# A two-layer diffusion block on one core: GpSimd keeps only powers, first weight pieces used two at a time, head norms in two steps

## The chip, the core and the metric

The kernel runs on one core of a Trainium2 chip. The core has five engines that run side by side: TensorE (PE in the profile) multiplies matrices, VectorE (DVE) and GpSimd (POOL) do arithmetic on tiles, ScalarE (ACT) does functions and copies, and SyncE (SP) issues DMAs. Each engine works through its own queue in order; semaphores hold an instruction until its inputs are there and its output buffer is free. The metric is device time in microseconds of one execution of the whole kernel.

## The reference

A stream of 256 latent tokens (`lat`) and one of 256 context tokens (`cx`), both 1024 wide, pass through two layers. Each layer is an FFN, a mixer and another FFN, each on the RMS-normed and modulated stream, with a gated addition behind it:

```python
for layer in range(DEPTH):                       # DEPTH = 2
    lat = macaron(lat, g[0], mod_l, 0, *f0)      # h + 0.5*gate*swiglu(adaln_in(h))
    cx = macaron(cx, g[0], mod_c, 0, *f0)
    h_l, h_c = adaln_in(lat, g[1], mod_l, 1), adaln_in(cx, g[1], mod_c, 1)
    y_l, y_c = mixer_ab(...) if layer % 2 == 0 else mixer_c(...)
    lat = macaron(lat + mod_l[:, 5] * y_l, g[2], mod_l, 2, *f1)
    if need_ctx:
        cx = macaron(cx + mod_c[:, 5] * y_c, g[2], mod_c, 2, *f1)
return rmsnorm(lat, final_norm_w)
```

`mixer_ab` (layer 0) has four heads of differential attention with rotary positions, whose outputs are RMS-normed per head (`rmsnorm(o, subln_w) * (1 - lam_init)`), and beside it a Hyena branch: a short convolution of three taps, then two long convolutions by Fourier transform with gates. `mixer_c` (layer 1) has 16 heads of neighbourhood attention with a position bias `rpb` on the latent keys. The modulation `mod` is a product of `silu(c)` with a 1024 x 9216 matrix in each layer. All data is float32.

## The kernel before

Tokens lie along the free axis: `res[d]` holds 128 channels of 512 tokens, latent in columns 0 to 255 and context in 256 to 511. Every float32 product is made of three products of a reduced type: `split` (L149) rounds a tensor to `hi` on ACT and takes `lo = src - hi` on another engine, and `mm3` (L154) issues hi*hi, hi*lo and lo*hi. Weights come in as raw tiles by DMA (`wload`, L494, three buffers) and are split in pieces of 128 output columns by `whalf` (L487) into the pools `whi` and `wlo`, four buffers each.

What the program writes is put into an order on each engine by a planner that has its own estimate of each instruction's cost; source order counts as priority. So neighbours in the source can be found mixed on an engine.

- **FFN** (`ffn`, L526). Eleven blocks of 256 hidden columns. For block 0, `ffn_first` (L521) loads w1 and w3 and makes four pieces (w1 and w3 of columns 0 to 127, then of 128 to 255), and `products` (L512) goes over the eight channel blocks k, all four pieces at each k, first for the latent stream, then for the context stream. Where `ffn` calls `ffn_first` itself, `lo` of these pieces is computed on GpSimd (L580). The very first FFN gets its pieces made earlier, on VectorE (L1087). The other blocks go piece by piece (`up`), and `down` adds the second product to `res` (L510).
- **Between blocks.** `after` is called behind the last products of each stream: `Adaln.stream` (L467) makes the next `h` from `res`. `token_rs` (L431) squares `res[d]` on ACT, adds up on VectorE (L439), sums over channels with matmuls by `ones` (L443, L444) and takes the power -1/2 on GpSimd (L447); `token_rstd` spreads it with a matmul (L455). `h` has eight buffers in the H pool.
- **mixer_ab** (L678). Projections alternate with heads of attention. `emit_qk` (L700) applies the rotation: multiplication by cos on GpSimd (L710), by sin on VectorE. `norms` (L863) norms two heads: squares and their sums (L868, L870), the power on GpSimd (L874), matmuls that spread it (L879), the product and its split. It is called for heads 0 and 1 behind `project_v` and the tables, and for heads 2 and 3 behind the first `spectrum`. `conv2` (L843) leaves its result in `zb`, four tiles of the H pool, which the last `out_project` reads. The M pool (six buffers) holds `v`, the tokens `vy` of the long convolutions, and the second FFN weights.
- **mixer_c** (L926). `position` (L960) loads a head's bias by two DMAs and adds the mask on GpSimd (L967), in the pool T of ten buffers; `scores` adds it to the scores on VectorE (L986).

Of the kernel before, what the change touches and what calls it, by code (L numbers as in the profile page):

```python
# [10 lines left out]
F32 = mybir.dt.float32  # L11
# [7 lines left out]
P = 128  # L19
# [78 lines left out]
def tile_dit(ctx: ExitStack, tc: tile.TileContext, a: dict, out: bass.AP, dbg=None):  # L98
# [49 lines left out]

    def split(hi, lo, src, eng=V):  # L149

        S.activation(hi, src, AF.Copy)  # L151
        eng.tensor_tensor(lo, src, hi.bitcast(F32), op=ALU.subtract)  # L152

# [332 lines left out]

    def whalf(src, name, shape=(8, P), eng=V):  # L487

        hi = wp.tile([P, *shape], F32R, tag="whi", name=name + "h")
        lo = wp.tile([P, *shape], F32R, tag="wlo", name=name + "l")  # L490
        split(hi, lo, src, eng)
        return hi, lo
# [27 lines left out]

    def ffn_first(l, j, eng=V):  # L521

        r1, r3 = [wload(a[nm][l, j][:, :FB]) for nm in ("ffn_w1", "ffn_w3")]
        return [whalf(r[:, :, P * c : P * c + P], "w", eng=eng) for c in range(2) for r in (r1, r3)]

    def ffn(l, j, streams, ad, mods, after, ws=None):  # L526
# [52 lines left out]
        n = len(streams)  # L579
        ws = ws or ffn_first(l, j, nc.gpsimd)  # L580
        first = [PU() for _ in range(4)]
        for s in streams:
            products(first, ws, h, span([s]))
        for b in range(NFB):
# [93 lines left out]
    def mixer_ab(ad, mods, after):  # L678
# [21 lines left out]
        def emit_qk(o):  # L700
            def emit(i, ps):
                i += o
                scale = 0.125 if i < 4 else 1.0
                hi, lo = qk[i] = G(name="qk")
                u, sw = X("u"), X("sw")
                S.activation(u, ps[:, :LAT], AF.Copy, scale=scale)
                S.activation(hi[:, LAT:], ps[:, LAT:], AF.Copy, scale=scale)
                V.scalar_tensor_tensor(lo[:, LAT:], ps[:, LAT:], scale, hi[:, LAT:].bitcast(F32), op0=ALU.mult, op1=ALU.subtract)
                V.stream_shuffle(sw, u, list(range(16, 32)) + list(range(16)))
                nc.gpsimd.tensor_tensor(u, u, cosT, op=ALU.mult)  # L710
                V.tensor_tensor(sw, sw, sinT, op=ALU.mult)
                V.tensor_tensor(u, u, sw, op=ALU.add)
                split(hi[:, :LAT], lo[:, :LAT], u)
            return emit
# [128 lines left out]
        def conv2(s, pinv=PS):  # L843
# [3 lines left out]
            for ch in range(4):  # L847
# [9 lines left out]
                if s == 0:  # L857
                    zb.append(H(name="z"))
                split(zb[ch][0][:, sl], zb[ch][1][:, sl], x)
# [3 lines left out]
        def norms(hds):  # L863
# [9 lines left out]
            V.tensor_scalar(rs[:, :n], st[:, :n], 1.0 / P, EPS, op0=ALU.mult, op1=ALU.add)  # L873
            nc.gpsimd.tensor_tensor(rs[:, :n], rs[:, :n], nhalf[:, :n], op=ALU.pow)  # L874
            for i, hd in enumerate(hds):
                bc = PS()
# [5 lines left out]
                za.append(G(name="z"))  # L882
                split(*za[hd], x)

        project_first(win, (0, 512), h, (emit_qk(0), emit_qk(4)))
# [9 lines left out]
        load_tokens("hv", 1)  # L895
        project(win, 1792, 2, h, emit_hy(2), PD)
        project_v(win, 1280, h, emit_v(1), PD)
        tab = [wp.tile([P, 2, TOK], F32R, tag=("whi", "wlo", "wlo")[i], name="tab") for i in range(3)]
# [3 lines left out]
        for o in range(2):  # L902
            nc.sync.dma_start(tn[o][1:], TR[o][0][1:])
            nc.sync.dma_start(tn[o][0:1], TN[o])
        norms((0, 1))
        head(2)
        project(win, 2048, 2, h, emit_hy(4), PD)
        head(3)
        load_filters(0)
        project(win, 2304, 2, h, emit_hy(6), PD)  # L910
        spectrum(PU, "hv", 0, 0)
        norms((2, 3))
        conv1(0)
# [12 lines left out]
    def mixer_c(ad, mods, after):  # L926
# [33 lines left out]
        def position(hd):  # L960
# [3 lines left out]
            for r2 in range(2):  # L964
                src = bass.AP(tensor=rpb.tensor, offset=hd * 465 + (5 - r2) * 31 - 48, ap=[[1, 64], [31, 6], [1, 64]])
                nc.sync.dma_start(b3[64 * r2 : 64 * r2 + 64], src)
            nc.gpsimd.tensor_tensor(b3, b3, mask, op=ALU.add)  # L967
            return b
# [192 lines left out]
```

## Time and profile before

| | us |
|---|---|
| median of 3 runs (1901.84 to 1902.35) | 1902.21 |
| the profiled execution | 1902.08 |
| its span | 1900.3 |
| PE busy | 1850.6 (97%) |
| VectorE busy | 1257.0 (66%) |
| ScalarE busy | 738.0 (39%) |
| GpSimd busy | 73.6 (4%) |

The profile has a row for each group of instructions: line of the kernel, engine, operation, tile names (out<-in), shapes, count, then busy time and mean duration in ns, then the engine's idle time in front of the group and what ended it. Views of single instructions give start and duration in us. A window's row gives the length, the busy time of PE, its weight loads, VectorE, ScalarE and GpSimd with instruction counts, and then the clock granted to TensorE as a share of full speed. A matmul's end is modelled, and matmuls overlap, so spacing from start to start tells more than duration.

### The profile page before, as it was taken

How to read it: one execution, taken by the hardware profiler on the slowest of the kernel's cores; microseconds unless marked ns; L12 is line 12 of the kernel's file. 1: busy time of each engine (PE TensorE's matmuls, PEld its weight loads, DVE VectorE, ACT ScalarE, POOL GpSimd, SP SyncE). 2: the span in 40 equal slices, each digit the busy share in tenths (PEclk: the TensorE clock that was granted, in tenths of full speed). 3: DMA queues.
4: the chain of work that ended last, by engine and by line, in shares of the span. 5: the costliest groups of instructions: out<-in, count | busy, mean ns of one | idle time of the engine just before them, and what ended most of it. 6: DMA issues, size and time to landing. Idle time of an engine off the chain costs nothing.

```text
span 1900.3 us, 25792 instructions
## 1 busy us (share of the span) xinstructions
PE 1850.6 (97%) x10358; PEld 1566.0 (82%) x10358; DVE 1257.0 (66%) x1972; ACT 738.0 (39%) x1190; POOL 73.6 (4%) x63
## 2 busy tenths in 40 slices
PE   7999999999999998999999999999999999989998
PEld 3868788889878788888888897887888988889998
DVE  5557686776666795877767358655344866667665
ACT  4533233224555433432332234222322566654443
POOL 1000000000100002000000110000000100020000
PEclk9999999999999999999999999999999999989998
DMA  8675555351323332545554325443323233335551
GB/s 267 216 245 177 171 186 208 127 191 45 122 88 100 104 109 84 195 170 175 197 184 143 111 78 176 173 160 113 111 89 119 54 106 84 106 111 178 200 188 57
DMA packets 191009, 271.65 MB, mean 143 GB/s; under 512 B 19688, under 2 KB 139755, under 8 KB 190889
## 3 DMA queue, kind: packets, MB, share of 16 engines
q1 hardware_dynamic: 189324, 267.63, 42.7%
q10 hardware_dynamic: 1260, 2.14, 0.3%
q8 instruction: 81, 1.33, 0.3%
q14 instruction: 40, 0.32, 0.1%
q0 software_dynamic: 304, 0.24, 0.0%
HBM read 262.63 MB, written 7.34 MB: 142 GB/s over the span
## 4 chain that ended last, share of the span: by engine, by line
PE 67%; DVE 4%; ACT 2%; issue 1%; POOL 1%; DMA 0%; SPq 0%; DVEq 0%; ACTq 0%
PE pu L155 11%; PE pu L156 11%; PE pu L157 11%; PE pd L155 7%; PE pd L157 7%; PE pd L156 7%; PE ps L155 3%; PE ps L156 3%; PE ps L157 3%; PE pu L1012 1%; DVE wl L152 1%; PE ps L667 1%; DVE acc L439 1%; PE pu L982 1%; PE ps L293 1%
## 5 line engine op out<-in xcount | busy, mean ns | idle before, releaser
L157 PE MATMUL pu<-h,wl 128*128 128x512 f32 (+1 forms) x1600 | 545.6, 342 | 3.0 <-POOL wl L152 3.0
L155 PE MATMUL pu<-h,wh 128*128 128x512 f32 (+1 forms) x1600 | 545.0, 342 | 1.6 <-ACT h L483 1.5
L156 PE MATMUL pu<-h,wh 128*128 128x512 f32 (+1 forms) x1600 | 546.0, 342 | 0.1
L151 ACT ACTIVATE wh<-raw 128x1024 fp32r<-128x1024 f32 x228 | 240.3, 1058 | 558.6 <-PE pu L156 403.2
L152 DVE TENSOR_TENSOR wl<-raw,wh 128x1024 fp32r<-128x1024 f32 x216 | 263.7, 1225 | 203.8 <-ACT wh L151 177.6
L155 PEld LDWEIGHTS pu<-h,wh 128*128 128x128 f32 x1600 | 303.8, 191 | 44.1 <-issue 4.2
L157 PEld LDWEIGHTS pu<-h,wl 128*128 128x128 f32 x1600 | 304.7, 191 | 38.4 <-POOL wl L152 3.3
L156 PEld LDWEIGHTS pu<-h,wh 128*128 128x128 f32 x1600 | 304.9, 191 | 33.8 <-DVE h L484 0.5
L282 DVE SCALAR_TENSOR_TENSOR mv<-mw,sF,mv 128x1024 f32<-128x1024 f32 x210 | 258.5, 1279 | 20.5 <-DMA mw<-in_mod_w_dram 16.2
L151 ACT ACTIVATE w<-raw 128x1024 fp32r<-128x1024 f32 x88 | 91.5, 1057 | 164.2 <-PE ps L156 120.5
L510 DVE SCALAR_TENSOR_TENSOR res<-pd,gate,res 128x256 f32<-128x256 f32 x244 | 110.7, 479 | 40.5 <-PE pd L157 40.0
L547 DVE TENSOR_TENSOR sg<-sg,pu 128x512 f32<-128x512 f32 (+1 forms) x87 | 52.2, 603 | 127.4 <-PE pu L157 125.0
L152 DVE TENSOR_TENSOR w<-raw,w 128x1024 fp32r<-128x1024 f32 x88 | 107.0, 1221 | 42.0 <-ACT w L151 41.9
L155 PE MATMUL pd<-g,w 128*128 128x512 f32 (+1 forms) x376 | 133.6, 355 | 0.0
L157 PE MATMUL pd<-g,w 128*128 128x512 f32 (+1 forms) x376 | 132.6, 353 | 0.0
L156 PE MATMUL pd<-g,w 128*128 128x512 f32 (+1 forms) x376 | 132.6, 353 | 0.0
L155 PE MATMUL ps<-g,w 128*128 128x512 f32 (+1 forms) x320 | 116.3, 363 | 0.0
L157 PE MATMUL ps<-g,w 128*128 128x512 f32 (+1 forms) x320 | 116.1, 363 | 0.0
L156 PE MATMUL ps<-g,w 128*128 128x512 f32 (+1 forms) x320 | 116.1, 363 | 0.0
L155 PE MATMUL pd<-h,wh 128*128 128x512 f32 (+1 forms) x288 | 108.3, 376 | 1.9 <-ACT e L989 0.9
L157 PE MATMUL pd<-h,wl 128*128 128x512 f32 (+1 forms) x288 | 107.6, 374 | 1.7 <-DVE wl L152 1.7
L156 PE MATMUL pd<-h,wh 128*128 128x512 f32 (+1 forms) x288 | 106.9, 371 | 0.0
(256 smaller groups left out, 2726.0 us busy)
## 6 DMA issues: line engine op xcount, KB each, us to landing
raw<-in_ffn_w_dram SPq DMA_DIRECT2D x132, 1024.0 KB, 5.3
mw<-in_mod_w_dram SPq DMA_DIRECT2D x144, 512.0 KB, 6.0
raw<-in_ab_w_in_dram SPq DMA_DIRECT2D x12, 1024.0 KB, 6.9
raw<-in_na_w_in_dram SPq DMA_DIRECT2D x12, 1024.0 KB, 5.0
raw<-in_ab_w_out_dram SPq DMA_DIRECT2D x4, 1024.0 KB
raw<-in_na_w_out_dram SPq DMA_DIRECT2D x4, 1024.0 KB, 5.5
bias<-in_na_rpb_dram SPq DMA_DIRECT2D x32, 96.0 KB, 6.1
dftr<-const_dft_dram SPq DMA_DIRECT2D x5, 256.0 KB
```

What stands on the lines that cost most here:

```text
L151: S.activation(hi, src, AF.Copy)
L152: eng.tensor_tensor(lo, src, hi.bitcast(F32), op=ALU.subtract)
L155: nc.tensor.matmul(ps, wh, xh, start=start, stop=False)
L156: nc.tensor.matmul(ps, wh, xl, start=False, stop=False)
L157: nc.tensor.matmul(ps, wl, xh, start=False, stop=stop)
L282: V.scalar_tensor_tensor(acc, mw, c, acc, op0=ALU.mult, op1=ALU.add)
L293: nc.tensor.matmul(ps[32 * j : 32 * j + 32], row[:, 31 - b : 63 - b], mod_acc[l, i][j % 2][:, j // 2], start=b == 0, stop=b == len(batch) ...
L439: V.tensor_tensor(acc, acc, q, op=ALU.add)
L510: V.scalar_tensor_tensor(res[d][:, sl], ps[:, po], g[:, d, s : s + 1], res[d][:, sl], op0=ALU.mult, op1=ALU.add)
L547: V.tensor_tensor(sg[:, sl], sg[:, sl], p3[:, sl], op=ALU.mult)
L667: nc.tensor.transpose(at[kt // 2][:, o : o + P], e[:, P * kt : P * kt + P], ident)
L982: nc.tensor.matmul(pss[m], x[pr, qsl], y[pr], start=n == 0, stop=n == 2)
```

## The change

`split`, `whalf` and `ffn_first` lose their engine parameter, so `lo` of the four first pieces of three FFNs is computed on VectorE; the multiplication by cos and the addition of the mask move there too. GpSimd then computes only the powers (L447, L874). The first products of an FFN go through two pieces (columns 0 to 127 of w1 and w3) for all k, then through the other two. `zb` is taken from the M pool. `norms` becomes a generator with two steps: squares, sums and power; then, at its second call, the spreading, product and split. The first step is now called one projection (`project_v`, or `project` at 2304 with a `spectrum`) ahead of the second, which stays in place.

```diff
--- before.py
+++ after.py
@@ -146,10 +146,10 @@
     V = nc.vector
     S = nc.scalar
 
-    def split(hi, lo, src, eng=V):
+    def split(hi, lo, src):
 
         S.activation(hi, src, AF.Copy)
-        eng.tensor_tensor(lo, src, hi.bitcast(F32), op=ALU.subtract)
+        V.tensor_tensor(lo, src, hi.bitcast(F32), op=ALU.subtract)
 
     def mm3(ps, wh, wl, xh, xl, start, stop):
         nc.tensor.matmul(ps, wh, xh, start=start, stop=False)
@@ -484,11 +484,11 @@
                 V.scalar_tensor_tensor(lo[:, sl], x, B, hi[:, sl].bitcast(F32), op0=ALU.add, op1=ALU.subtract)
 
 
-    def whalf(src, name, shape=(8, P), eng=V):
+    def whalf(src, name, shape=(8, P)):
 
         hi = wp.tile([P, *shape], F32R, tag="whi", name=name + "h")
         lo = wp.tile([P, *shape], F32R, tag="wlo", name=name + "l")
-        split(hi, lo, src, eng)
+        split(hi, lo, src)
         return hi, lo
 
     def wload(src):
@@ -518,10 +518,10 @@
     def span(streams):
         return slice(LAT * streams[0], LAT * streams[-1] + LAT)
 
-    def ffn_first(l, j, eng=V):
+    def ffn_first(l, j):
 
         r1, r3 = [wload(a[nm][l, j][:, :FB]) for nm in ("ffn_w1", "ffn_w3")]
-        return [whalf(r[:, :, P * c : P * c + P], "w", eng=eng) for c in range(2) for r in (r1, r3)]
+        return [whalf(r[:, :, P * c : P * c + P], "w") for c in range(2) for r in (r1, r3)]
 
     def ffn(l, j, streams, ad, mods, after, ws=None):
         h = ad.h
@@ -577,10 +577,11 @@
 
         raws, gs = {}, {}
         n = len(streams)
-        ws = ws or ffn_first(l, j, nc.gpsimd)
+        ws = ws or ffn_first(l, j)
         first = [PU() for _ in range(4)]
         for s in streams:
-            products(first, ws, h, span([s]))
+            for c in range(2):
+                products(first[2 * c : 2 * c + 2], ws[2 * c : 2 * c + 2], h, span([s]))
         for b in range(NFB):
             if b > 0:
                 raws[b] = [wload(w[:, FB * b : FB * b + FB]) for w in (w1, w3)]
@@ -707,7 +708,7 @@
                 S.activation(hi[:, LAT:], ps[:, LAT:], AF.Copy, scale=scale)
                 V.scalar_tensor_tensor(lo[:, LAT:], ps[:, LAT:], scale, hi[:, LAT:].bitcast(F32), op0=ALU.mult, op1=ALU.subtract)
                 V.stream_shuffle(sw, u, list(range(16, 32)) + list(range(16)))
-                nc.gpsimd.tensor_tensor(u, u, cosT, op=ALU.mult)
+                V.tensor_tensor(u, u, cosT, op=ALU.mult)
                 V.tensor_tensor(sw, sw, sinT, op=ALU.mult)
                 V.tensor_tensor(u, u, sw, op=ALU.add)
                 split(hi[:, :LAT], lo[:, :LAT], u)
@@ -855,7 +856,7 @@
                 nc.sync.dma_start(x, X2[ch][:, sl])
                 V.tensor_tensor(x, x, ps[:, :LAT], op=ALU.mult)
                 if s == 0:
-                    zb.append(H(name="z"))
+                    zb.append(M(name="z"))
                 split(zb[ch][0][:, sl], zb[ch][1][:, sl], x)
 
         za = []
@@ -872,6 +873,7 @@
             rs = sp.tile([P, 16], F32, tag="rs16", name="rs16")
             V.tensor_scalar(rs[:, :n], st[:, :n], 1.0 / P, EPS, op0=ALU.mult, op1=ALU.add)
             nc.gpsimd.tensor_tensor(rs[:, :n], rs[:, :n], nhalf[:, :n], op=ALU.pow)
+            yield
             for i, hd in enumerate(hds):
                 bc = PS()
                 for t in range(4):
@@ -881,6 +883,9 @@
                 V.scalar_tensor_tensor(x, oT[hd], sub8, bc, op0=ALU.mult, op1=ALU.mult)
                 za.append(G(name="z"))
                 split(*za[hd], x)
+            yield
+
+        norm = [norms((0, 1)), norms((2, 3))]
 
         project_first(win, (0, 512), h, (emit_qk(0), emit_qk(4)))
         project(win, 1536, 2, h, emit_hy(0), PD)
@@ -894,6 +899,7 @@
         project(win, 256, 2, h, emit_qk(2), PD)
         load_tokens("hv", 1)
         project(win, 1792, 2, h, emit_hy(2), PD)
+        next(norm[0])
         project_v(win, 1280, h, emit_v(1), PD)
         tab = [wp.tile([P, 2, TOK], F32R, tag=("whi", "wlo", "wlo")[i], name="tab") for i in range(3)]
         tables(3, lambda i: tab[i][:, 0], lambda i: tab[i][:, 1])
@@ -902,14 +908,15 @@
         for o in range(2):
             nc.sync.dma_start(tn[o][1:], TR[o][0][1:])
             nc.sync.dma_start(tn[o][0:1], TN[o])
-        norms((0, 1))
+        next(norm[0])
         head(2)
         project(win, 2048, 2, h, emit_hy(4), PD)
         head(3)
         load_filters(0)
+        next(norm[1])
         project(win, 2304, 2, h, emit_hy(6), PD)
         spectrum(PU, "hv", 0, 0)
-        norms((2, 3))
+        next(norm[1])
         conv1(0)
         spectrum(PU, "hv", 1, 0)
         load_filters(1)
@@ -964,7 +971,7 @@
             for r2 in range(2):
                 src = bass.AP(tensor=rpb.tensor, offset=hd * 465 + (5 - r2) * 31 - 48, ap=[[1, 64], [31, 6], [1, 64]])
                 nc.sync.dma_start(b3[64 * r2 : 64 * r2 + 64], src)
-            nc.gpsimd.tensor_tensor(b3, b3, mask, op=ALU.add)
+            V.tensor_tensor(b3, b3, mask, op=ALU.add)
             return b
 
         def scores(half, i):
```

## The prediction

> **What bounds the kernel now.** I read the page's busy table first, then its groups, then the waits of PE, then windows around the places where PE is idle.
>
> ```profile
> PE 1850.6 (97%) x10358; PEld 1566.0 (82%) x10358; DVE 1257.0 (66%) x1972; ACT 738.0 (39%) x1190; POOL 73.6 (4%) x63
> L155 PE MATMUL pu<-h,wh 128*128 128x512 f32 (+1 forms) x1600 | 545.0, 342 | 1.6 <-ACT h L483 1.5
> ```
>
> PE is busy 97% of the span and nearly always with the three matmuls of `mm3`, which the change neither adds to nor removes. So the change can only move the other 3%, and the clock that PE is granted. Where that lies shows in windows (columns: length, then busy us of PE, PEld, DVE, ACT, POOL, then granted clock, DMA share, GB/s).
>
> ```profile
> 430.00:470.00 40.00, 38.46 (x314) 37.43 (x313) 29.01 (x74) 19.79 (x42) 1.40 (x2) 1.00 0.16 52
> 700.00:770.00 70.00, 63.28 (x423) 58.10 (x422) 45.10 (x86) 28.71 (x54) 12.78 (x6) 0.98 0.26 87
> 1095.00:1130.00 35.00, 32.39 (x250) 30.78 (x249) 23.98 (x57) 15.25 (x35) 6.20 (x4) 0.95 0.31 106
> 1675.00:1712.00 37.00, 30.79 (x215) 28.84 (x214) 24.61 (x50) 19.64 (x34) 10.21 (x5) 0.86 0.28 92
> ```
>
> Each is a passage from one block to the next: squares, `token_rs`, `stream`, first products. The first leads into `mixer_ab`, whose first pieces are already split on DVE; it leaves PE idle 40 - 38.46 = 1.5 us. The other three lead into the FFNs that call `ffn_first(l, j, nc.gpsimd)`: call them A (700 to 770, idle 6.7), B (1095 to 1130, idle 2.6) and C (1675 to 1712, one stream only, idle 6.2). What ended the idle time in A and C, from the timelines of PE, DVE, POOL and ACT:
>
> ```profile
> 712.11 2.39 POOL L152 TENSOR_TENSOR wl<-raw,wh 128x1024 fp32r<-128x1024 f32 x1 [63.85 <-DVE res L510]
> 717.55 2.37 POOL L152 TENSOR_TENSOR wl<-raw,wh 128x1024 fp32r<-128x1024 f32 x1 [3.04 <-ACT wh L151]
> 717.81 2.38 DVE L439 TENSOR_TENSOR acc<-acc,sq 128x256 f32<-128x256 f32 x1 [0.29 <-ACT sq L437]
> 720.64 0.39 PE L155 MATMUL pd<-z,wh 128*128 128x256 f32 x1 [1.89 <-DVE res L510]
> 732.31 4.18 POOL L152 TENSOR_TENSOR wl<-raw,wh 128x1024 fp32r<-128x1024 f32 x1 [4.08 <-ACT wh L151]
> 736.55 0.47 PE L157 MATMUL pu<-h,wl 128*128 128x256 f32 x1 [3.05 <-POOL wl L152]
> 740.74 1.71 ACT L483 ACTIVATE h<-xr,modT 128x256 fp32r<-128x256 f32 x4 [6.96 <-PE pd L157]
> 1684.79 2.62 DVE L439 TENSOR_TENSOR acc<-acc,sq 128x256 f32<-128x256 f32 x2 [0.15 <-ACT sq L437]
> 1688.25 0.39 PE L155 MATMUL pd<-z,wh 128*128 128x256 f32 x1 [2.35 <-DVE res L510]
> L439 DVE TENSOR_TENSOR acc<-acc,sq x72: 406/425/2416, 14.4 to 1889.8; 128x256 f32<-128x256 f32 x72
> ```
>
> The addition of L439 takes 425 ns as a rule and 2.38 us while a POOL split runs, and ends with it: a DVE instruction with both inputs in SBUF stands still until POOL is done. Behind it waits the `res` addition that frees PE's accumulator, hence 1.89 us in A and 2.35 us in C. The third POOL split of A takes 4.18 us, held in turn by DVE, and PE, which needs all four pieces at k = 0, waits 3.05 us. The ACT row is the H pool: `h` of d = 4 to 7 waits until the last `out_project` matmul has let go of `zb`.
>
> **The change part by part.** Splits, and `zb`:
>
> ```profile
> L152 POOL TENSOR_TENSOR wl<-raw,wh 128x1024 fp32r<-128x1024 f32 x12 | 30.5, 2542 | 468.7 <-ACT wh L151 403.8 <-DVE res L510 63.8 <-PE pd L157 1.1
> L152 DVE TENSOR_TENSOR wl<-raw,wh 128x1024 fp32r<-128x1024 f32 x216 | 263.7, 1225 | 203.8 <-ACT wh L151 177.6 <-PE pu L157 13.9 <-PE pu L982 10.5
> 736.50:741.50 5.00, 4.95 (x29) 4.96 (x30) 0.92 (x3) 0.76 (x2) 0.00 (x0) 0.66 0.67 210
> 1108.00:1112.00 4.00, 3.62 (x19) 3.40 (x20) 1.77 (x6) 0.69 (x2) 0.70 (x1) 0.59 0.58 232
> 1470.00:1515.00 45.00, 44.21 (x349) 43.09 (x350) 34.84 (x78) 23.69 (x51) 5.61 (x6) 0.96 0.25 64
> ```
>
> POOL loses 12 x 2542 ns, DVE gains 12 x 1225 ns = 14.7 us. In A I take the idle time of the passage that already has four DVE splits: 6.7 - 1.5 = 5.2 us gained. After the 3.05 us stop the clock is 0.66 for 5 us, so 5 x 0.34 = 1.7 us more goes. Moving `zb` to the M pool frees the H buffers earlier; the six M buffers hold only `hz` tokens by then, which end before `conv2`, so I cost it at nothing, and its gain is inside the 5.2. In B: 2.6 - 1.5 = 1.1 us, and of its clock loss (0.41 x 4 = 1.6) half, 0.8, since the passage at 1470, without POOL splits, also shows 0.96; bounds 0 and 1.6. In C there is no second stream to hide the chain, so only the held time: 2.62 us for two additions instead of 0.85, 1.8 us, and 0.5 us of its clock loss (bounds 0 and the whole 0.14 x 37 = 5.2; near the low end, as the chain that idles PE stays). Against it, four splits of 1.2 us come between C's `res` additions on DVE: bounds 0 and 4.9, I take one, 1.2.
>
> Two at a time: PE takes 6 instead of 12 matmuls of each `h[k]` before the next, so `h` must come faster. Its price and its gain:
>
> ```profile
> 1694.53 1.28 DVE L482 SCALAR_TENSOR_TENSOR xr<-res,A,bs 128x256 f32<-128x256 f32 x3 [2.51 <-ACT bs L457]
> 1695.72 1.27 DVE L484 SCALAR_TENSOR_TENSOR h<-xr,modT,h 128x256 fp32r<-128x256 f32 x3
> 733.10 0.28 PE L155 MATMUL pu<-h,wh 128*128 128x256 f32 x1
> 733.22 0.28 PE L156 MATMUL pu<-h,wh 128*128 128x256 f32 x1
> PE pd L157 <- DVE wl L152: 1.7, 4, 0.5
> ```
>
> DVE makes three `h` in 2.4 us by the starts of these groups, 0.8 us each; six matmuls of 256 columns, 0.12 us from start to start, take 0.72 us. Eight times 0.08 is 0.6, with the start 0.8 us, paid in C alone (bounds 0 and 2). The gain: pieces 1 and 2 come free 48 matmuls before the end of the first products, so the next block's first split no longer waits for that end. The wait above occurs four times; three follow an FFN's first products (0.5, 0.5 and, in C, 0.2 us), the fourth, 0.5, follows `project_first` and stays: 1.2 us.
>
> Head norms:
>
> ```profile
> L874 POOL TENSOR_TENSOR rs<-rs,nhalf 128x8 f32<-128x8 f32 x2 | 3.6, 1824 | 76.6 <-DVE rs L873 76.6
> 592.65 0.60 PE L879 MATMUL ps<-cst,rs 128*128 128x128 f32 x3 [1.33 <-POOL rs L874]
> 648.32 0.58 PE L879 MATMUL ps<-cst,rs 128*128 128x128 f32 x1 [1.85 <-POOL rs L874]
> 646.00:650.00 4.00, 2.15 (x10) 1.72 (x10) 0.77 (x2) 0.00 (x0) 2.01 (x1) 0.74 0.16 59
> 650.00:654.00 4.00, 4.00 (x21) 3.56 (x21) 2.90 (x5) 1.26 (x2) 0.00 (x0) 0.83 0.00 0
> ```
>
> PE stands 1.33 and 1.85 us in front of the broadcasts, and after the second the clock costs 4 x 0.26 + 4 x 0.17 = 1.7 us. With `project_v`, or `project` and `spectrum`, between the power and its use, all of it has cover: 3.2 + 1.7 = 4.9 us. The 32 broadcasts stay. Without cover the row says 1.8 us each.
>
> Bias and rope onto DVE:
>
> ```profile
> L967 POOL TENSOR_TENSOR bias<-bias,cst 128x384 f32<-128x384 f32 x16 | 17.2, 1083 | 471.4 <-DMA bias<-in_na_rpb_dram 427.7 <-DVE z L152 43.7
> 1539.70:1551.90 12.20, 12.20 (x63) 9.96 (x62) 5.84 (x10) 4.71 (x10) 3.37 (x4) 1.00 0.65 132
> 1540.00:1560.00 20.00, 20.00 (x122) 17.02 (x123) 11.94 (x24) 9.27 (x20) 4.19 (x4) 1.00 0.54 128
> 1539.70 6.80 SPq L966 DMA_DIRECT2D bias<-in_na_rpb_dram  x8
> 1551.86 0.86 POOL L967 TENSOR_TENSOR bias<-bias,cst 128x384 f32<-128x384 f32 x1 [0.96 <-DMA bias<-in_na_rpb_dram]
> 1555.31 0.76 DVE L986 TENSOR_TENSOR pu<-pu,bias 128x256 f32<-128x256 f32 x2
> L547 DVE TENSOR_TENSOR sg<-sg,pu 128x512 f32<-128x512 f32 x60 | 41.0, 685 | 83.8 <-PE pu L157 83.0 <-ACT sg L546 0.7
> L711 DVE TENSOR_TENSOR sw<-sw,rope 128x256 f32<-128x256 f32 x8 | 4.4, 544 | 0.1
> 476.00:500.00 24.00, 22.02 (x102) 17.79 (x101) 20.44 (x39) 13.17 (x25) 5.65 (x5) 1.00 0.49 153
> ```
>
> No row has 128x384 on DVE. Between L439's 425 ns (256 columns) and L547's 685 ns (512 columns) I take 0.55 us: 16 x 0.55 = 8.8 us, four to each half. Around a batch DVE has 8.1 of 20 us free and PE is busy throughout, so the work itself is hidden. Not so a wait: POOL waited for the bias DMAs and nobody behind it cared; on DVE the split of `k` and the next `wl` stand behind. I take 0.5 us for each of four batches, 2.0 (bounds 0 and 23; see the third rival; nearer to nothing, as the DMAs are issued 15 us before the first L986 of the half, 1555.31). Rope: 8 x 0.43 = 3.4 us more on DVE; POOL's products lengthened L711 from 425 to 544 ns, 8 x 0.12 = 1.0 us that goes again. 476 to 500 is DVE's fullest stretch here (20.4 of 24) and PE idles 2.0 in it; net 2.4, of which 0.7 on the path (bounds -1 and 2.4).
>
> Gains 6.9 (A) + 1.9 (B) + 2.3 (C) + 4.9 (norms) + 1.2 (pieces) = 17.2; costs 1.2 + 0.8 + 2.0 + 0.7 = 4.7. Net 12.5 us. The profiled execution took 1902.1 us, 1.8 around its span of 1900.3, and the median shown is 1902.2; so **1889.6 us**. Moving work between engines also changes the order laid out on all of them; that has no row, and I leave it in the range as 4 us either way.
>
> **The rivals.**
> First, DVE becomes the late engine at the passages: it does one thing at a time, and in A it is busy 45 of 70 us. If half of each of the 12 splits falls on the path, 12 x 0.61 = 7.3 instead of 1.2: net 6.4, 1895.7 us. Against it stands the passage at 430, which has such splits and idles 1.5.
>
> Second, the change doesn't do what it says: engines do not run in source order (matmuls of `z` stand among those of `h` in A), so the planner may put the norms' second step next to the first again, and mix the four pieces. Then 4.9 + 1.2 - 0.8 = 5.3 falls away: 1894.9 us.
>
> Third, slower: the bias additions stand at the head of DVE's queue before their data are there. In the batch above, SP issues from 1539.7 on and the last addition starts at 1551.86: 12.2 us, in which DVE does 5.84 us of other work. If it stood still all that time, those 5.84 us would be late for `k` and the scores behind them: 23.4 us in four batches instead of 2.0, so 1889.6 + 21.4 = 1911.0 us. The time turns slower than before from (12.5 + 2.0) / 4 = 3.6 us a batch. Against it stands the 15 us between the issue and the use. [...]
>
> Fourth, the clock stays as it is, because it is low wherever PE has thin stretches, stalls or not: 0.96 at the 1470 passage with PE idle only 0.8 us. Then 1.7 + 0.8 + 0.5 + 1.7 = 4.7 us of the gain fall away: 1894.3 us. [...]
>
> **How the numbers follow.** Forecast 0.54, first rival 0.17, second 0.08, third 0.07, fourth 0.14. The range 1883 to 1899 holds all but the third: its low end is no costs at all (1884.9) and some of C's clock besides, its high end the first or fourth rival with the reordering's 4 us against it. 0.2% is 3.8 us, about what a measurement of this kernel tells from no change; the first two and the fourth gain more than that, less their tails: faster 0.85, same 0.08 (two rivals together), slower 0.07.
>
> **What would show it.** Right: no L439 or L484 above 0.5 us at the passages, PE idle near 1.5 to 2.5 in A and B, no PE wait on L874, granted clock near 1.00 behind the norms. Wrong: DVE waits on bias DMAs of several us with PE waits in `scores`; PE waits on DVE `wl` at the first products; PE idle at 476 to 500 clearly above 2 us.

## The result and the profile after

The changed kernel takes 1891.43 us (median of 4 runs, 1888.69 to 1892.94) beside 1902.03 us before (1901.81 to 1902.35): ratio 0.9937, 95% interval 0.9925 to 0.9949, so 10.6 us less. The forecast was 1889.6 us in a range of 1883 to 1899. The profiled execution is the fastest of the four, 1888.69 us with a span of 1886.9 us, 13.4 us shorter than the one before.

The busy table of the changed kernel:

```profile
PE 1844.3 (98%) x10358; PEld 1558.9 (83%) x10358; DVE 1268.1 (67%) x2008; ACT 739.2 (39%) x1190; POOL 16.7 (1%) x27
```

VectorE took over 12 splits, 16 mask additions and 8 products; these are its rows, with the additions of L439 and the product by sin (now L712). The last row is that of L439 in the kernel before:

```profile
L152 DVE TENSOR_TENSOR wl<-raw,wh 128x1024 fp32r<-128x1024 f32 x228 | 278.6, 1223 | 195.3 <-ACT wh L151 178.4 <-PE pu L157 8.5 <-PE pu L989 5.1
L439 DVE TENSOR_TENSOR acc<-acc,sq 128x256 f32<-128x256 f32 x72 | 30.3, 421 | 4.9 <-ACT sq L437 2.3
L974 DVE TENSOR_TENSOR bias<-bias,cst 128x384 f32<-128x384 f32 x16 | 8.6, 556 | 5.2 <-DMA bias<-in_na_rpb_dram 5.1
L711 DVE TENSOR_TENSOR u<-u,rope 128x256 f32<-128x256 f32 x8 | 3.4, 423 | 0.1
L712 DVE TENSOR_TENSOR sw<-sw,rope 128x256 f32<-128x256 f32 x8 | 3.4, 420 | 0.0
L439 DVE TENSOR_TENSOR acc<-acc,sq 128x256 f32<-128x256 f32 x72 | 37.3, 518 | 7.3 <-ACT sq L437 4.0 <-DVE acc L439 0.5
```

That is 12 x 1.22 + 8.6 + 3.4 = 26.7 us of new work, yet VectorE is busy only 11.1 us longer (1257.0 before). Most of the other 15.6 us is time in which its own instructions had stood still beside a GpSimd one. Four rows show 11.9 us of it: L439 fell from 518 ns on average to 421 (7.0 us), the splits of `g` of 256 columns from 515 to 420 (2.7), those of `qk` behind the rotation from 578 to 421 (1.3) and the product by sin from 544 to 420 (1.0). The rest has no row. Not every VectorE instruction was held: beside GpSimd's pieces in the kernel before, L510, which reads PE's accumulator, kept its 468 to 485 ns, and so did L482 (479 ns) beside the piece of 4.18 us.

The waits of PE in the changed kernel (total, times, longest):

```profile
PE ps L259 <- DMA mw<-in_mod_w_dram: 8.6, 3, 6.2
...
PE pd L155 <- DVE res L510: 2.9, 5, 1.0
PE ps L443 <- DVE acc L439: 1.5, 3, 1.1
...
PE ps L155 <- ACT y L151: 1.3, 2, 0.7
...
PE pd L157 <- DVE wl L152: 0.5, 1, 0.5
```

The waits on the powers of the norms (3.2 us before) and on GpSimd's pieces (3.0) are gone, and those for the next block's piece are down from four (1.7 us) to one. The wait on `mw` has grown from 2.9 us (longest 2.3) to 8.6 (longest 6.2), and those on `y` are new. Windows of the changed kernel, first the place of the `mw` wait, then the old passages, moved by the time gained so far (columns as in the prediction):

```profile
80.00:100.00 20.00, 13.76 (x74) 8.74 (x74) 7.22 (x8) 6.03 (x8) 0.00 (x0) 0.83 0.44 144
...
480.00:504.00 24.00, 23.47 (x114) 19.18 (x113) 20.62 (x45) 13.80 (x25) 0.00 (x0) 1.00 0.42 129
700.00:764.00 64.00, 62.94 (x425) 57.74 (x425) 46.51 (x89) 28.12 (x52) 1.39 (x2) 1.00 0.29 96
1089.00:1122.00 33.00, 31.87 (x256) 30.28 (x255) 24.60 (x60) 15.10 (x36) 1.39 (x2) 1.00 0.29 97
1470.00:1506.00 36.00, 34.93 (x280) 33.29 (x281) 29.84 (x72) 20.50 (x45) 1.40 (x2) 1.00 0.19 59
1660.00:1700.00 40.00, 33.66 (x247) 32.00 (x248) 31.49 (x60) 22.51 (x38) 0.70 (x1) 0.91 0.35 113
```

A and B idle 1.1 us each at full clock; C still idles 6.3 us at 0.91. The first window has a counterpart in the kernel before, with PE idle 0.5 instead of 6.2 us:

```profile
80.00:100.00 20.00, 19.47 (x108) 13.78 (x106) 8.26 (x9) 7.45 (x10) 0.00 (x0) 1.00 0.47 145
```

Windows shift between kernels, so I also compared them **at equal PE work**: in each trace the columns of the matmuls were added up in order of start (3,967,824 in every kernel, the 145 matmuls of fewer than 64 columns counted as 64, a choice of the author's), and the times at which two kernels had reached the same sum were subtracted. The table gives, for each stretch of the kernel before, how many us a kernel's profiled execution needed more or less than that of before. e1 to e12 are the experiments below.

| stretch of before, us | 0-80 start | 80-120 mw | 120-475 | 475-520 rope | 520-575 | 575-680 norms | 680-700 conv2 | 700-790 A | 790-1170 B | 1170-1570 bias | 1570-end C | sum |
|---|---|---|---|---|---|---|---|---|---|---|---|---|
| predicted | 0 | -0.5 | 0 | +0.7 | 0 | -4.9 | 0 | -7.4 | -1.9 | +2.0 | -0.5 | -12.5 |
| changed | -1.0 | +6.9 | -0.4 | -1.7 | -0.4 | -3.7 | +2.1 | -7.9 | -3.1 | -2.1 | -2.3 | -13.5 |
| e12 changed again | +1.4 | +7.5 | -0.4 | -1.6 | -0.4 | -3.8 | +3.6 | -7.8 | -3.1 | -2.2 | -2.1 | -8.9 |
| e1 four in first FFN | -0.3 | 0.0 | 0.0 | -1.7 | -0.1 | -3.8 | +3.6 | -7.8 | -3.1 | -2.2 | -1.2 | -16.7 |
| e2 GpSimd pieces | +6.1 | +7.5 | -0.4 | -1.7 | -0.5 | -3.8 | +3.6 | -4.3 | -0.3 | -2.2 | +0.1 | +4.1 |
| e3 norms together | -1.2 | +7.0 | +1.2 | -1.7 | -0.5 | +1.7 | +2.1 | -7.8 | -3.1 | -2.2 | -2.1 | -6.7 |
| e4 zb in H | -1.0 | +5.6 | -0.4 | -1.7 | -0.4 | -3.8 | 0.0 | -7.2 | -3.1 | -2.2 | -2.2 | -16.2 |
| e5 e1 and e4 | -1.1 | 0.0 | 0.0 | -1.6 | -0.2 | -3.8 | 0.0 | -7.2 | -3.1 | -2.2 | -2.1 | -21.1 |
| e6 bias on GpSimd | 0.0 | +7.1 | -0.4 | -1.7 | -0.5 | -3.8 | +3.6 | -7.9 | -3.1 | -0.5 | -2.1 | -9.2 |
| e7 rope on GpSimd | +0.9 | +7.3 | -0.4 | 0.0 | +0.3 | -3.9 | +2.1 | -7.8 | -3.1 | -1.3 | -2.2 | -8.1 |
| e8 four everywhere | +2.6 | 0.0 | +0.2 | -1.7 | -0.2 | -3.8 | +3.6 | -6.8 | -2.8 | -2.2 | -1.5 | -12.6 |
| e9 before + two | +2.5 | +7.2 | -0.4 | 0.0 | +0.2 | -0.3 | 0.0 | 0.0 | +0.1 | -0.2 | 0.0 | +9.2 |
| e10 before + splits | +0.9 | +0.1 | 0.0 | 0.0 | 0.0 | -0.1 | 0.0 | -6.1 | -2.8 | -0.8 | -1.5 | -10.2 |
| e11 e5 and halves | -0.8 | +0.2 | +2.0 | -1.7 | -0.2 | -3.8 | 0.0 | -7.2 | -3.1 | -2.2 | -1.5 | -18.1 |

In the row "predicted" the 1.2 us of the pieces are laid to the first FFN, A and C (0.5, 0.5, 0.2): the four waits of the kernel before start at 88.2, 477.5 (the one of `project_first`), 764.6 and 1709.4 us, and none follows the first products at B. C's two costs are laid to C. The columns repeat to 0.2 us in most kernels that share the edit. The exceptions are the start, `mw`, `conv2` and C, the column 120-475 in e3 and e11, and two columns of e7; more on them below. Of the column C only the part up to 1720 us is the passage: -1.7 us in the changed kernel, -2.0 in e12, -0.2 in e1, +1.1 in e2, -1.1 in e4, -2.0 in e5, -0.6 in e8, -1.0 in e10 and -0.4 in e11. The rest, 0.1 to 1.1 us, comes in the last matmuls of the kernel, which no edit touches and where the granted clock falls to 0.50 at different moments (9.9 us before the end of the span in the kernel before, 9.0 us in the changed one).

### The profile page after: what moved, and what is told of

The parts are those of the page before. It is cut to its first block, busy times and chain, and to the rows that moved or that the text cites. A ratio compares the mean times of both kernels' runs of the same rounds, so it can differ in the third digit from the quotient of the medians.

```text
span 1886.9 us, 25716 instructions
## 1 busy us (share of the span) xinstructions
PE 1844.3 (98%) x10358; PEld 1558.9 (83%) x10358; DVE 1268.1 (67%) x2008; ACT 739.2 (39%) x1190; POOL 16.7 (1%) x27
## 4 chain that ended last, share of the span: by engine, by line
PE 90%; DVE 4%; DMA 3%; ACT 2%; issue 1%; POOL 0%; SPq 0%; ACTq 0%; DVEq 0%
PE pu L155 16%; PE pu L156 16%; PE pu L157 15%; PE pd L155 9%; PE pd L156 9%; PE pd L157 9%; PE ps L155 4%; PE ps L157 4%; PE ps L156 4%; DMA mw<-in_mod_w_dram 1%; PE ps L293 1%; PE ps L259 1%; DVE wl L152 1%; PE pu L1019 1%; PE ps L668 1%
## 5 line engine op out<-in xcount | busy, mean ns | idle before, releaser
L152 DVE TENSOR_TENSOR wl<-raw,wh 128x1024 fp32r<-128x1024 f32 x228 | 278.6, 1223 | 195.3 <-ACT wh L151 178.4
L510 DVE SCALAR_TENSOR_TENSOR res<-pd,gate,res 128x256 f32<-128x256 f32 x244 | 110.6, 479 | 41.0 <-PE pd L157 40.2
L152 DVE TENSOR_TENSOR w<-raw,w 128x1024 fp32r<-128x1024 f32 x88 | 106.9, 1221 | 42.7 <-ACT w L151 42.7
```

Source lines behind the costliest of these rows:

```text
L152: V.tensor_tensor(lo, src, hi.bitcast(F32), op=ALU.subtract)
L510: V.scalar_tensor_tensor(res[d][:, sl], ps[:, po], g[:, d, s : s + 1], res[d][:, sl], op0=ALU.mult, op1=ALU.add)
```

## The experiments

| kernel | median, us | before beside it | ratio, 95% interval |
|---|---|---|---|
| e1 four in the first FFN | 1887.78 | 1903.36 | 0.991, 0.9895 to 0.9925 |
| e2 pieces on GpSimd | 1902.81 | 1903.36 | 0.9995, 0.9985 to 1.0006 |
| e3 norms together | 1895.09 | 1903.36 | 0.9948, 0.9928 to 0.9968 |
| e4 zb in H | 1888.66 | 1903.36 | 0.9914, 0.9899 to 0.9929 |
| e5 e1 and e4 | 1884.13 | 1903.07 | 0.9899, 0.9882 to 0.9915 |
| e6 bias on GpSimd | 1893.90 | 1903.07 | 0.9949, 0.9931 to 0.9967 |
| e7 rope on GpSimd | 1893.81 | 1903.07 | 0.995, 0.9933 to 0.9967 |
| e8 four everywhere | 1888.20 | 1903.07 | 0.9917, 0.9897 to 0.9936 |
| e9 before + two in the first FFN | 1910.55 | 1903.57 | 1.0036, 1.0022 to 1.005 |
| e10 before + splits on VectorE | 1892.98 | 1903.57 | 0.9943, 0.993 to 0.9956 |
| e11 e5 and halves | 1883.93 | 1903.57 | 0.9897, 0.9885 to 0.991 |
| e12 changed, again | 1892.30 | 1903.57 | 0.9935, 0.9922 to 0.9949 |

The intervals are 2 to 4 us wide to each side, so single effects are read at equal PE work, and the medians say whether they add up.

### The wait on mw: e1, e9

In the changed kernel PE starts the second pair of the first block and then stands (PE's timeline, then SP's):

```profile
85.82 0.39 PE L155 MATMUL pd<-h,wh 128*128 128x512 f32 x1
...
92.46 1.07 PE L259 MATMUL ps<-mw,sF 128*32 128x512 f32 x2 [6.24 <-DMA mw<-in_mod_w_dram]
```

```profile
77.56 0.24 SPq L909 DMA_DIRECT2D tn<-TR  x1
77.89 3.53 SPq L910 DMA_DIRECT2D tn<-TN  x1
81.51 13.78 SPq L256 DMA_DIRECT2D mw<-in_mod_w_dram  x5
```

SP issues `mw` only at 81.51 us, behind the loads of `tn`; the matmul that needs it stands one place behind the first `pd`. e1 gives the first FFN alone its old order of use:

```diff
-            for c in range(2):
+            for c in range(2) if (l, j) != (0, 0) else ():
                 products(first[2 * c : 2 * c + 2], ws[2 * c : 2 * c + 2], h, span([s]))
+            if (l, j) == (0, 0):
+                products(first, ws, h, span([s]))
```

> The changed kernel, but the very first FFN goes through its first four pieces together again, as before the change; the other three FFNs keep two at a time. Theory: with two pieces at a time PE's queue in the first FFN puts the modulation matmuls of L259 one matmul behind the start of the first products, in front of mw data that SP issues only at 81.5 us; the 6.2 us wait at 85.8 to 92.5 us comes from that order alone. Then the wait on mw falls to 0 to 1 us, the broadcast before mixer_ab (447 us) comes 5 to 6 us earlier, the median is 1884 to 1887 us, and the runs lie within 1 us of each other as before the change, since no DMA's arrival decides any more. Rival: the wait comes from the new order of SP's queue, where the loads of tf and tn stand in front of mw; then it stays, and the time is 1890 to 1893 us.

The stretch 80-120 falls from +6.9 to 0.0 us; in e1's window PE idles 0.5 us:

```profile
80.00:100.00 20.00, 19.47 (x107) 13.59 (x107) 8.25 (x9) 7.45 (x10) 0.00 (x0) 1.00 0.48 146
```

In e1 24 matmuls of `pd` stand ahead of the first of L259, in the changed kernel one. The gain was as expected in its stretch (the median is 0.8 us over the expected band, beside a before that is 1.3 us slower here too). The spread was not: the runs lie between 1885.84 and 1888.85 us, so it has another source (see the last section). e9 makes the converse edit, two at a time for `(l, j) == (0, 0)` only, in the kernel before:

> The kernel before with one edit: the very first FFN uses its first four pieces two at a time. Theory: the order of PE's queue there is enough to make the wait on mw; the modulation matmuls of L259 come one matmul behind the first product and PE waits 5 to 7 us for mw at 86 us, so that the time is 5 to 7 us over that of the kernel before, 1907 to 1910 us beside 1902 to 1903. Rival: it needs the changed kernel's other edits as well; then the time is that of before.

The wait appears with this edit alone, 7.2 us in the stretch, and the runs are 7.0 us slower than before. PE's wait in e9:

```profile
PE ps L259 <- DMA mw<-in_mod_w_dram: 8.7, 3, 5.8
```

The rival, a new order of SP's queue, is out: in the kernel before and in e1 the loads of `tf` and `tn` stand in front of `mw` in the same order, and `mw` is issued no earlier (from 82.28 and 82.04 us on). So cause and size are settled: the planner's order on PE, not the new place of any load.

### Where zb lies: e4

```diff
-                    zb.append(M(name="z"))
+                    zb.append(H(name="z"))
```

> The changed kernel with zb in the H pool again. Theory: h of d = 4 to 7 of the FFN behind mixer_ab waits until the last matmul of the output projection has let go of zb, which the trace before showed as 6.96 us of ACT idle at 740.7 us; PE has the other half of h to work on, with two pieces at a time for only half as long, so passage A (700 to 764 us) loses 1 to 4 us and nothing else moves. Rival: with the DVE splits in place the wait is hidden, and the time is within 0.5 us of the changed kernel.

The theory's sign was wrong for the kernel: e4 loses 0.7 us in A, less than the 1 to 4 expected, and wins 2.1 us in `conv2`, where the theory expected nothing. The changed kernel's PE there:

```profile
693.60 0.39 PE L157 MATMUL pd<-z,wl 128*128 128x512 f32 x1
693.82 0.28 PE L155 MATMUL ps<-tab,y 128*128 128x256 f32 x1
...
695.43 0.39 PE L155 MATMUL ps<-tab,y 128*128 128x256 f32 x1 [0.73 <-ACT y L151]
...
696.15 0.38 PE L157 MATMUL ps<-tab,y 128*128 128x256 f32 x1 [0.22 <-DVE y L152]
```

Counted in the two traces, 8 matmuls of the output projection (`pd`) stand between the first and the second batch of `conv2` in the changed kernel, 15 in e4, and e4's second batch waits for nothing. So with `zb` in the M pool the planner sets the second batch of `conv2` earlier than its inputs `y` allow. Why it does so is not shown.

### The engine of the first pieces: e2, e10, and the order of their use: e8

e2 gives `split`, `whalf` and `ffn_first` their engine parameter back, and `ffn` calls `ffn_first(l, j, nc.gpsimd)`. e10 is the kernel before with `ws = ws or ffn_first(l, j)`, so VectorE makes the pieces and all else is old. e8 uses `products(first, ws, h, span([s]))` in all FFNs.

> The changed kernel with lo of the first four pieces of three FFNs on GpSimd again (pieces still used two at a time). Theory: the additions of L439 stand still again for over 2 us while a GpSimd split runs, and A, B and C lose what they gained, less the wait at 736 us for all four pieces, which two at a time halves: 4 to 9 us slower than the changed kernel, 1895 to 1900 us, of it 2 to 5 in A, 1 to 2 in B and 1 to 2 in C. Rival: the gain at the passages came from the new order of use and from zb, not from the engine; then the time is within 2 us of the changed kernel.

> The kernel before with one edit: lo of the first pieces of the three FFNs on VectorE, still used four at a time, zb still in the H pool. Theory: the splits' engine alone brings nearly all that the passages gained, at equal PE work 5.5 to 7.5 us in A (700 to 780 us), 2.5 to 3 us in B (1100 to 1160 us) and 0 to 2 us in C (1660 to 1720 us, where a change of the granted clock of up to 1.5 us comes and goes between executions): 8 to 12 us faster than before. Rival: without two at a time PE still waits for the third and fourth piece in A; then A gains 2 to 4 us.

> The changed kernel with the first four pieces used together in all four FFNs, so the two-at-a-time part is undone and the rest stays. Theory: the first FFN gains 5.9 us as with four at a time there alone; at A, B and C the order of use changes little, since VectorE has all four pieces ready: the waits for wl at the second block come back (0.5, 0.5 and 0.2 us) and h can come slower, so 0 to 1.5 us lie between this kernel and the one with four at a time only in the first FFN. Rival: part of the gain at A (7.9 us at equal PE work) was two at a time, which lets PE begin before the third and fourth piece; then A loses 1 to 3 us.

Beside the changed kernel e2 loses 3.6 us in A, 2.8 in B and 2.8 in C up to 1720 us, 9.2 us together, just over the 4 to 9 expected; B and C lie above their parts of it (1 to 2 each). Its median, 1902.81 us, lies 3 us over the expected band and back at that of before. e10 alone has -6.1 in A, -2.8 in B and -1.0 in C up to 1720 us, 9.9 us in all, beside 10.6 by the medians. The changed kernel gains 12.7 us in the three passages, so most of it is the splits' engine. (e10's -0.8 in the bias column, which its edit does not touch, is clock: the kernel before runs at half clock for 3.4 us from 1487.6 us on, e10 does not.) e8 gives A -6.8 and B -2.8 instead of -7.8 and -3.1: two at a time is worth 1.3 us there, e4 makes `zb` worth 0.7 in A, and 6.1 + 1.0 + 0.7 = 7.8 us closes the sum of A. e8's rival, 1 to 3 us in A, was right at its low end. In C up to 1720 us e8 gains 1.1 us less than the changed kernel, but it has one more interval at half clock there (see the last section), so the order of use is not separated from the clock in C. e10's first two windows, A and B, and its third, C:

```profile
700.00:766.00 66.00, 63.65 (x434) 58.40 (x434) 46.34 (x94) 29.87 (x55) 1.40 (x2) 1.00 0.28 93
1090.00:1122.00 32.00, 30.87 (x247) 29.29 (x247) 23.68 (x58) 14.29 (x33) 1.40 (x2) 1.00 0.35 116
1665.00:1702.00 37.00, 30.75 (x221) 28.88 (x221) 27.46 (x54) 20.55 (x36) 0.71 (x1) 0.91 0.32 105
```

### Head norms: e3

```diff
         project(win, 1792, 2, h, emit_hy(2), PD)
-        next(norm[0])
...
+        next(norm[0])
         next(norm[0])
         head(2)
```

and the same for heads 2 and 3.

> The changed kernel with both steps of the norms called together at the old places, so that nothing stands between the power and its spreading. Theory: PE waits 1.3 and 1.8 us in front of the two spreadings again and the clock is lost behind them: 4 to 6 us slower than the changed kernel, between 437 and 728 us of the span only. Rival: the 5.8 us that mixer_ab gained came from the rotation on VectorE and from the order; then it is at most 2 us slower.

From 575 to 680 us e3 needs 1.7 us more than the kernel before and 5.4 more than the changed one, in line with the theory. The 1.7 us over the kernel before come with one more 3.4 us at half clock: e3 has two, from 597.5 and 655.5 us on, the kernel before one, from 648.0 on. Its window behind the second power shows both parts, the wait and the clock:

```profile
652.00:656.00 4.00, 2.15 (x14) 1.72 (x14) 0.77 (x2) 0.00 (x0) 2.01 (x1) 0.94 0.26 92
656.00:660.00 4.00, 4.00 (x17) 3.52 (x16) 2.96 (x5) 1.26 (x2) 0.00 (x0) 0.64 0.00 0
```

The medians say 0.9948 beside 0.9937 and 0.9935 for the changed kernel, with overlapping intervals; they neither support nor exclude 5 us.

### Bias and rope: e6, e7

Each puts one `V.tensor_tensor` back to `nc.gpsimd.tensor_tensor`: e6 that of the mask (L974), e7 that of the cos (L711).

> The changed kernel with the mask addition of position on GpSimd again. At equal PE work the changed kernel wins 2.1 us between 1480 and 1560 us, where no first piece is split, instead of losing the 2.0 us that the prediction charged. Theory: the sixteen additions on VectorE cost nothing that PE sees, because their DMAs come early enough, and the 2.1 us come from the shorter stalls and order at the passage into mixer_c; then this kernel keeps them and is within 1 us of the changed one. Rival 1: the additions on GpSimd hold VectorE as the splits did, so this kernel loses 1 to 2 us of the 2.1. Rival 2: the waits on the bias DMAs do cost VectorE's followers, and this kernel is 1 to 2 us faster.

> The changed kernel with the product by cos on GpSimd again. At equal PE work the changed kernel wins 1.6 us between 480 and 500 us, where the prediction charged 0.7. Theory: with the product on GpSimd PE waits for cv at 488 us again (L774, 1.6 us before) because GpSimd's products hold VectorE's own in the fullest stretch; this kernel loses 1.2 to 2 us there and nothing elsewhere. Rival: the planner's order made the difference; then less than 0.5 us is lost there.

e7: the stretch 475-520 goes from -1.7 to 0.0 us, and PE's wait for `cv` (1.6 us in all) is back. "Nothing elsewhere" did not hold: e7 also loses 0.7 us in 520-575 and 0.8 in the bias column, for reasons that were not traced. GpSimd's products hold the one by sin, 543 ns instead of 420:

```profile
L712 DVE TENSOR_TENSOR sw<-sw,rope 128x256 f32<-128x256 f32 x8 | 4.3, 543 | 0.1
```

In e7 VectorE is busy 1268.1 us, as in the changed kernel: the 3.4 us of moved products cost it nothing. e6: 1170-1570 goes from -2.1 to -0.5 us, the number of rival 1, but not by its mechanism. PE's waits in e6 and in the changed kernel differ here:

```profile
PE pu L1019 <- DVE al L152: 1.1, 2, 0.6
...
PE pd L155 <- ACT e L996: 0.8, 1, 0.8
```

```profile
PE pu L1019 <- DVE al L152: 0.5, 1, 0.5
...
PE pd L155 <- ACT e L996: 0.2, 1, 0.2
```

e6's stalls lie at 1515 to 1531 us, while its GpSimd does nothing between 1495.6 and 1539.6 us. So no holding by GpSimd makes them. The planner lays the queues otherwise when the additions are elsewhere, and that order is what is left as a cause; it is argued here and not shown by a run.

### The same kernel twice: e12

> The changed kernel once more, nothing edited, to see what two executions of one program differ by and to have it beside the best version on one chip. Theory: at equal PE work it differs from its first profile only where PE stands for 0.5 to 2 us and the granted clock does or doesn't fall behind it (steps of 1 to 1.6 us at 466, 695 and 1680 us), and where PE waits for the mw DMAs; all other stretches agree within 0.1 us. The median is 1890 to 1895 us, and 5 to 9 us above the version with four at a time and zb in H. Rival: the differences between the kernels at those three places are the kernels' own; then this profile shows what the first one did within 0.3 us.

The theory held, with a larger share at the start. Of the 4.6 us between the two profiles, 2.4 lie before 80 us (granted clock 0.66 instead of 0.83 in 30 to 40 us), 0.6 at `mw` and 1.5 in `conv2`. There the stops are the same and the clock behind them is not. The first fence has e12's 5 us with the stops and the 5 us behind them, the second the first profile's 5 us with most of the stops (behind them its clock is 1.00, as in the window from 700 us above):

```profile
694.00:699.00 5.00, 4.24 (x26) 3.49 (x25) 4.86 (x9) 2.77 (x4) 0.00 (x0) 1.00 0.03 3
699.00:704.00 5.00, 4.49 (x23) 4.29 (x24) 4.72 (x13) 1.67 (x4) 0.00 (x0) 0.68 0.07 23
```

```profile
695.00:700.00 5.00, 4.04 (x29) 3.62 (x30) 4.86 (x13) 2.31 (x6) 0.00 (x0) 1.00 0.08 26
```

C behaves alike: e1 and e5 have the same stops to within 0.1 us, and up to 1720 us e1 needs 1.8 us more, with 10.2 us at half clock there instead of 6.8. The last section shows where these differences come from.

### Versions that are better: e5, e11

> Both single improvements together: the very first FFN with its first four pieces together, and zb in the H pool. Theory: the two places are far apart, so the parts add: no wait on mw above 2.5 us at 85 us (5.9 us), no wait of PE on y of conv2 near 690 us (2.1 us, or 3.6 with the clock as in the kernel with four at a time), 0.7 us less gained at passage A; median 1883 to 1886 us beside a before of 1902 to 1903, the profiled span 1880 to 1883 us, ratio near 0.990. Rival: what one of them gains was the chance of one execution or comes back as a wait elsewhere; then it is no faster than the better of the two (ratio 0.991).

e5 holds to the theory in every stretch: 0.0 at `mw`, 0.0 in `conv2`, -7.2 in A. Its median is 1884.13 us, ratio 0.9899 with an interval of 0.9882 to 0.9915, which lies below that of the changed kernel. e11 adds to it, for the last FFN:

```diff
-        split(hi, lo, src)
+        for k in ((0, 4), (4, 8)) if halves else ((0, shape[0]),):
+            split(hi[:, k[0] : k[1]], lo[:, k[0] : k[1]], src[:, k[0] : k[1]])
```

> The best version so far (the very first FFN with four pieces together, zb in the H pool) and one more edit: in the last FFN each first piece is split in two halves of four channel blocks, so that eight instructions of about 0.65 us stand between the res additions on VectorE instead of four of 1.22 us. Theory: the stalls of PE at C, 1.15, 0.66, 0.42, 0.89 and 1.30 us, in which PE waits for a res or acc addition behind such a split, get shorter by 1 to 2 us in all. Rival: the additions are late for other reasons, and eight splits with their own fixed cost take as much; then C stays within 0.5 us.

The rival is right in its mechanism (in the changed kernel L152 takes 686 ns for 512 columns of `g` and 1223 for 1024 of `wl`). From start to start, PE's stops at C add up to 4.4 us in five pieces with whole splits (0.42 to 1.30 us each) and to 4.4 us in eight with halves (0.33 to 1.27 us). The ratio, 0.9897, is that of e5. Up to 1720 us C is even 1.6 us worse than in e5, with 10.2 us at half clock instead of 6.8, and so is 120-475, by 2.0 us, with 3.4 us at half clock from 461.6 us on. C's single stream leaves PE waiting for the chain itself.

## Why the prediction was right, and where it was not

The forecast was 1889.6 us, 1.8 us under the median. The largest term, the splits, was right in its mechanism, but this closeness is in part luck: errors of several us cancel.

- **Splits.** Right in mechanism and nearly in size: A 7.9 (7.4 predicted with its piece), B 3.1 (1.9). L439 is at 421 ns, POOL's pieces are gone from the waits, and the clock in both passages is 1.00. Taking `mixer_ab`'s passage as the yardstick for the idle time worked. Half of B's clock loss was too little: e10 gains 2.8 us there, which is the 1.1 of idle time and the whole of the clock loss (3.4 us at half clock, 1.7 us).
- **zb.** The step "I cost it at nothing, and its gain is inside the 5.2" failed. The 5.2 us needed no `zb` (e10); the move itself gained 0.7 us in A and lost 2.1 us in `conv2` (e4), by an order that the sum did not look at.
- **C.** -1.7 us up to 1720 us for -0.5, and most of the difference is clock. Without its 0.5 for the clock the sum gives 0.0 in C. e1, e8 and e11, which spend the same 10.2 us at half clock there as the kernel before, gain 0.2 to 0.6; the changed kernel spends 6.8, and 3.4 us at half clock are up to 1.7 us. Which of the two an execution gets is the luck of the last section. The 0.8 for `h` was too high: PE waits for it once in C, 1.5 us, before as after. Halving the splits between the `res` additions only moves the stops (e11), so the 1.2 for them stays untested.
- **Norms.** -3.7 for -4.9 beside the kernel before, 5.4 beside e3. PE no longer waits on L875 at all, so the cover was there. Part of the missing 1.2 us are two stops of 0.5 and 0.7 us, from start to start, at 622 and 663 us.
- **Pieces.** Three of four waits went, as forecast, in the first FFN, A and C. Two at a time gained 1.3 us in A and B.
- **Bias.** The step "0.5 us for each of four batches, 2.0" had the wrong sign. VectorE waits three times, 5.1 us in all, for the bias DMAs, and no wait of PE there grows by more than 0.1 us; of the column's 2.1 us the move wins 1.6 (e6). The third rival fell with it: its waits exist, at no price that PE shows.
- **Rope.** "0.7 of which on the path" had the wrong sign too: 1.7 us won. The held product was seen and priced (1.0 us). That the moved products would add nothing to VectorE's busy time (1268.1 us with them and without, e7), and that PE's wait for `cv`, 1.6 us, would go with the move, was not. How much of that is the end of the holding and how much a new order is not separated.
- **Order.** The step "that has no row, and I leave it in the range as 4 us either way" is the one that failed most: two at a time in the first FFN alone costs 7 us (e9), by a matmul of L259 that the planner put in front of its data, and `conv2` 2 us more (e4). The time stayed inside the range because the bias column (4.1 us), rope (2.4) and C (1.2 up to 1720 us) came out better than forecast.
- **The other rivals.** The first (VectorE late) is refuted in A and B by PE's single remaining wait of 0.5 us on `wl`, the second (planner undoes the steps) by the missing waits on L875. Of the fourth, "the clock stays", A, B and the norms show the opposite, all at 1.00; only C stays at 0.91. This is no luck of one execution. Beyond the stops of `conv2`, none of the eleven traces with these splits on VectorE has a stretch at half clock in A or B, and each of the three with GpSimd's (the kernel before, e2, e9) has at least one. Between 575 and 680 us none of the ten traces with the norms in two separated steps has one, and all four others do. The passage at 1470, also at 1.00 now, says nothing: it is so in e10 too, where nothing was changed there.

## What to carry to other kernels

Before work is moved off GpSimd, look for VectorE instructions that take far longer than their group's usual time (here L439, both inputs in SBUF: up to 2.42 us beside a GpSimd split, 425 ns as a rule). Here 11.9 us of such time came back in four rows, and the moved products cost VectorE nothing (e7). Where a planner lays out the queues, a change of loop order or of a buffer pool is also a change of order, and its price can exceed that of the edit's visible terms; look for what a queue is late with near each touched place (here DMAs issued at 81.5 us) and try each such edit alone. Compare two kernels at equal work rather than at equal time, and profile one of them twice before a difference of 1 to 2 us is believed. Count the stretches at half clock in each trace first: here each 3.4 us of them can account for up to 1.7 us.

## What the runs showed that was not expected

A stop of PE of less than 1 us can cost 1.5 us of clock behind it or nothing, in programs that are the same up to that point. In the traces this goes with the stop's place in time. Each trace keeps the granted clock as steps, and in all 14 it is either 1.00 or 0.50. Before the last 50 us each of the 55 stretches at 0.50 lasts one, two, three or four times 3.41 us. In the kernel before they start at 33.56, 647.96, 736.70, 1108.76, 1487.63 and 1689.02 us, in the changed kernel at 31.31, 89.34 and 1679.95. Within a trace all steps lie on one grid of 3.41 us, and the place of this grid beside the program differs from execution to execution, even of one kernel.

The changed kernel and e3 have the same order and the same two stops at 464 to 467 us (0.27 and 0.7 us, from start to start). These are the grid's intervals there, first two of the changed kernel, then two of e3:

```profile
464.80:468.21 3.41, 2.77 (x22) 2.56 (x22) 0.23 (x2) 0.38 (x1) 0.69 (x1) 1.00 0.00 0
468.21:471.62 3.41, 3.41 (x31) 3.41 (x30) 3.38 (x9) 1.79 (x5) 0.00 (x0) 1.00 0.00 0
```

```profile
464.36:467.77 3.41, 2.77 (x22) 2.37 (x21) 0.58 (x2) 0.00 (x0) 0.69 (x1) 1.00 0.00 0
467.77:471.18 3.41, 3.41 (x18) 3.41 (x18) 2.98 (x8) 1.77 (x5) 0.00 (x0) 0.50 0.00 0
```

In e3 PE does 18 matmuls in the second interval instead of 31, which is the 1.5 us by which it falls back there. e3's first interval holds both stops (matmuls start at 464.49 and 464.89, at 466.24 and 467.04). In the changed kernel the boundary at 464.80 cuts off the first one (464.53 to 464.92). Five other traces have the same two stops with a boundary in or between them (e2, e4, e6, e7, e12), and none loses clock there. The stops of `conv2` near 695 us (1.01, 0.50 and 0.59 us from start to start) behave alike. In e1, e2, e6, e8 and e12 their idle time lies, to 0.1 us, within one interval, and the next one is at 0.50. In the changed kernel, e3 and e7 a boundary cuts off a part (the last 0.2 us in the changed kernel), and the clock stays at 1.00. So the stop is the program's and its price is the luck of the execution. How much standing within an interval it takes is not shown: a stop at 592 us in the kernel before, 1.48 us beyond the usual spacing and within one interval, cost no clock, and e3's of 1.14 us at 597 us did.

In e3's interval ahead of the fall PE was busy for 2.77 of the 3.41 us, so PE did not stand for a whole interval there. Such steps, at 466, 695 and 1680 us and at the start, are of the size of the spread between runs of one kernel (1887.39 to 1893.27 us in e12); that they make up all of it is not shown.
